# High and low part of the tokens in one matmul: a decoder layer in split precision on one core of Trainium2

## The chip, the core and the metric

The kernel runs on one core of a Trainium2 chip. The core has a matrix engine (TensorE, PE in the profile; its weight loads are shown apart as PEld), three engines for element-wise work (VectorE or DVE, ScalarE or ACT, GpSimd or POOL) and a queue that issues most transfers (SyncE, SP). Matmuls read on-chip memory and write accumulators that lie in eight banks of 512 float32 values in each of 128 partitions. Each engine carries out its own instructions in the order in which the program writes them, and waits for others by semaphores. The metric is device time in microseconds (us), lower is better. Before the change three runs took 393.45 to 395.39, with a median of 394.48.

## What is computed

One decoder layer over 256 tokens of width 1024, float32, with 256 memory tokens: half of the first projection goes through a causal pooling mixer, the other half through self-attention with 8 heads of 64 (256 tokens are one block, so it is plain causal attention); then cross-attention with 4 heads of 256 into the memory, then a gated feed-forward layer of width 2816. Each of the three parts ends in a residual sum and a layer normalisation.

```python
z = h @ w_in[l]
u, q, k, v = ...          # 512 columns each
pool_out = multiscale_pool(u, w_pool[l], pool_scale[l])
attn_out = moba_attention(q, k, v).reshape(B_, S_, ATTN_WIDTH)
mix = jnp.concatenate([pool_out, attn_out], axis=-1) @ w_out[l]
h = layer_norm(DEEPNORM_ALPHA * h + mix, ln1_g[l], ln1_b[l])
h = layer_norm(DEEPNORM_ALPHA * h + memory_cross_attention(h, mem, w_xq[l], w_xkv[l], w_xo[l]), ...)
h = layer_norm(DEEPNORM_ALPHA * h + swiglu(h, w_gate[l], w_up[l], w_down[l]), ...)
```

## The kernel before

**Split precision.** Every large product is made of three matmuls of a faster, rounded float32 type (fp32r). A matrix is split into a high part (a rounded copy, made by ACT) and a low part (what rounding left, made by DVE); the three products are high x high, high x low and low x high, and low x low is left out. They are summed in one accumulator.

**Weights.** `Stream` (L42) brings weights in pieces of 512 KB, numbered w0, w1, ... in the order of their use. `fetch` issues the transfer, and `prepare` makes the high part on ACT (L79) and the low part on DVE (L80). `get` prepares what is asked for and, unless `held` is set, one more piece, up to six ahead (`AHEAD`). There are four raw buffers and eight pairs of prepared ones. Other transfers hang on pieces through `before`: the transposed tokens `xr`, the memory `mr`, the residual `xt`, the norms' parameters. w0 to w8 belong to q and k, w9 to w12 to v, w13 to w16 to u, w17 to w24 to the memory's keys.

**Two kinds of product.** In `proj_rows` and `proj_n` a block of tokens is stationary, and high and low part of the weights stream past it. In `proj_t` and `product_qk` a block of 128 x 128 weights is stationary and the 256 tokens stream, so that the result comes out transposed. For each block of weights these issue three matmuls of 256 columns: high weights with high tokens, high weights with low tokens, low weights with high tokens. High and low tokens lie in two separate tiles (`xT`, `mT`, `cT`, `h1T`, `h2T`, ...), each of 8 blocks of 256 tokens.

**Accumulators.** Two pools share the eight banks: `accbank` gives one of four single banks for long products, `bank` one of four for everything else (scores, transposes, attention). A transposed product of 256 channels fills one bank: two times 256 tokens.

**The order.** It is written out by hand. After q and k (`product_qk`, L315, emptied by `keep_qk`, L303) the generators `do_v`, `do_u` and `do_xk` (L446 to L467) are advanced step by step (`run(v, 2)` makes two steps), and the pieces of self-attention are put in between: `scores` (L373, scores, mask, row maximum on DVE, exponentials on ACT, scaling on DVE), `probs_t` (L395, transposes of the probabilities and their copies, one on DVE, one on ACT), `attend` (L411), then `windows` (L424, on POOL), `pool_diff` and `mix_pool` for pooling. What leaves an accumulator is issued when its generator is advanced past its last step: u's first half, for instance, is copied (L457) after `scores(1, 1)` and `attend(1)`, as its sixteenth step lies behind them. The cross-attention follows the same pattern: `do_xq` (L619) makes the queries of one head, split into high and low by L280 and L281, and `xscores` of that head comes five or six steps into the next head's queries. Gate and up (L730) are ten rounds of two transposed products; `project` (L564) makes the three products that end in a residual sum.

Of the kernel before, what the change touches and what calls it, by code (L numbers as in the profile page):

```python
# [14 lines left out]
P = 128  # L15
# [18 lines left out]
PR_BUFS = 6  # L34
BUSY = 13
# [68 lines left out]
def decoder_layer(  # L104
# [8 lines left out]
    pa = ctx.enter_context(tc.tile_pool(name="pacc", bufs=4, space=bass.MemoryType.PSUM))  # L113
# [5 lines left out]

    def bank(name):  # L120
# [29 lines left out]
    xT = (a8("xTh", F32R), a8("xTl", F32R))  # L150
    mT = (a8("mTh", F32R), a8("mTl", F32R))
# [6 lines left out]
    def load_xt(k, n=2):  # L158
        nc.sync.dma_start(xr[:, k:k + n, :], x_t[:, k:k + n, :])

    def split_xt(k, n=2):
        split(xT[0][:, k:k + n, :], xT[1][:, k:k + n, :], xr[:, k:k + n, :])
# [7 lines left out]
    def split_mem(k):  # L170
        split(mT[0][:, k:k + 4, :], mT[1][:, k:k + 4, :], mr[0][:, k:k + 4, :])
# [56 lines left out]
    def proj_t(pss, numbers, yT, last=True):  # L228

        for f in range(2):  # L230
            for k in range(KD):
                hi, lo = ws.get(numbers, k)
                s = slice(f * P, (f + 1) * P)
                three(pss[f], (hi[:, s], lo[:, s]), pair(yT, ALL, k), k == 0, k == KD - 1)
                if f == 1 and last:
                    ws.done(numbers, k)
                yield

    def proj_n(ps, numbers, yT, t, last=True):

        for k in range(KD):
            three(ps, pair(yT, ALL, k, slice(t * P, (t + 1) * P)), ws.get(numbers, k), k == 0, k == KD - 1)
# [4 lines left out]
    def proj_rows(acc, chunks, get, pieces, first, last, free):  # L247
# [3 lines left out]
        for numbers in chunks:  # L251
            nk = ws.rows(numbers)
            for t in sorted({piece[0] for piece in pieces}):
                for j in range(nk):
                    k = k0 + j
                    y = pair(get(k), ALL, slice(t * P, (t + 1) * P))
# [26 lines left out]
    def transpose_tok(dst, tok, t, k0):  # L283
# [5 lines left out]
        split(dst[0][:, k0:k0 + 4, ts], dst[1][:, k0:k0 + 4, ts], ps.rearrange("p (k t) -> p k t", k=4))  # L289
# [11 lines left out]
    qk = [accbank(f"pqk{i}").rearrange("p (f t) -> p f t", f=2) for i in range(4)]  # L301

    def keep_qk(i):  # L303

        dst = qkT[:, 2 * i:2 * i + 2, :]
        if i == 0:
            nc.scalar.mul(dst, qk[i], HD ** -0.5)
        elif i == 1:
            nc.vector.tensor_scalar(dst, qk[i], HD ** -0.5, None, op0=OP.mult)
        elif i == 2:  # L310
            nc.scalar.copy(dst, qk[i])
        else:
            nc.vector.tensor_copy(dst, qk[i])

    def product_qk(k):  # L315
        for i in range(4):
            j, c0 = divmod(i, 2)
            hi, lo = ws.get(c_qk[k], j)
            for f in range(2):
                s = slice((2 * c0 + f) * P, (2 * c0 + f + 1) * P)  # L320
                (ya, yb), (wa, wb) = pair(xT, ALL, k), (hi[:, s], lo[:, s])
                for n, (w, y) in enumerate(((wa, ya), (wa, yb), (wb, ya))):
                    nc.tensor.matmul(qk[i][:, f, :], w, y, start=k == 0 and f == 0 and n == 0,  # L323
                                     stop=k == KD - 1 and n == 2, skip_group_check=True)
            if k == KD - 1:
                keep_qk(i)
# [33 lines left out]
    def scaled(dst, sm):  # L360
        nc.vector.reciprocal(sm, sm)  # L361
        for j in range(2):
            nc.vector.tensor_scalar(dst[:, j, :], dst[:, j, :], sm[:, j:j + 1], None, op0=OP.mult)  # L363
# [9 lines left out]
    def scores(hq, t):  # L373
# [15 lines left out]
        for pr, sm in todo:  # L389
            scaled(pr, sm)  # L390

    cT = (a8("cTh", F32R), a8("cTl", F32R))
# [18 lines left out]
    def attend(hp):  # L411
# [7 lines left out]
        split(cT[0][:, 4 + hp, :], cT[1][:, 4 + hp, :], po[:, :S])  # L419
# [18 lines left out]
    def mix_pool(g):  # L438
        pm = bank("pm")
        nc.tensor.matmul(pm[:, :S], wpl[:, g, :], upad[:, g, PADW:], start=True, stop=True)  # L440
        nc.scalar.activation(cT[0][:, g, :], pm[:, :S], AF.Copy, bias=0.0, scale=psc[:, g:g + 1])
        nc.vector.scalar_tensor_tensor(cT[1][:, g, :], pm[:, :S], psc[:, g:g + 1],
                                       r32(cT[0][:, g, :]), op0=OP.mult, op1=OP.subtract)
# [358 lines left out]
```

## Time and profile before

| | us |
|---|---|
| median of three runs | 394.48 (393.45 to 395.39) |
| the profiled execution | 393.67 |
| its span, first to last instruction | 391.6 |
| TensorE busy in it | 381.3 (97%) |
| VectorE busy | 244.6 (62%) |
| ScalarE busy | 176.1 (45%) |
| transfers | 72.0 MB, 184 GB/s on average |

The mean clock granted to TensorE is 0.996 of full speed. In the timelines that follow, a row has the start in us, the length in us, the engine, the line of the kernel, the operation, result and operands by the names of the program, shapes, type and count; what stands in brackets is how long the engine was idle before, and what ended that. Recorded lengths of matmuls overlap. Rows of stages begin with the stretch in us, then its length, the busy time of PE, PEld, DVE, ACT and POOL with the number of instructions, the granted clock, the share of the DMA engines and GB/s.

### The profile page before, as it was taken

Reading aid. Unit: us, or ns where it says so; the run is one execution under the profiler, and the core shown is the slowest. Engines: PE = TensorE matmul, PEld = TensorE weight load, DVE = VectorE, ACT = ScalarE, POOL = GpSimd, SP = SyncE. Lnnn points to the kernel's source line nnn. Section 1 sums busy time; section 2 is a strip of 40 time slices with the busy share of each in tenths; the row PEclk is TensorE's granted clock in tenths of the full one; section 3 lists DMA queues with packets and bytes.
Section 4 is the critical chain, followed back from the end, with each engine's and each line's share of the span. In section 5 each row is a group of like instructions: output and inputs, shape, how many; then the busy total and the mean of one; then the engine's idle time right before and its main releaser. Section 6 shows DMA issues by size and latency. Waiting matters only on the chain.

```text
span 391.6 us, 6504 instructions
## 1 busy us (share of the span) xinstructions
PE 381.3 (97%) x2651; PEld 353.6 (90%) x2651; DVE 244.6 (62%) x327; ACT 176.1 (45%) x253; POOL 31.0 (8%) x37
## 2 busy tenths in 40 slices
PE   8999999999999999999999999999999999999991
PEld 7997889898888899988899999999999998888881
DVE  2749998776388766656887744556644457543276
ACT  3745848455233645455245633355543335343000
POOL 1000006500420000001400000000000000000022
PEclk9999999999999999999999999999999999999998
DMA  7998544756606862234408756654445875753002
GB/s 239 336 329 273 200 166 148 273 174 228 236 9 220 281 251 109 110 107 161 162 3 279 241 177 216 216 179 173 144 170 197 277 258 163 256 175 108 1 27 82
DMA packets 21886, 71.99 MB, mean 184 GB/s; under 512 B 2784, under 2 KB 3552, under 8 KB 21728
## 3 DMA queue, kind: packets, MB, share of 16 engines
q1 hardware_dynamic: 21568, 71.05, 52.7%
q10 hardware_dynamic: 288, 0.52, 0.7%
q8 instruction: 21, 0.34, 0.3%
q14 instruction: 9, 0.07, 0.1%
HBM read 70.52 MB, written 1.05 MB: 183 GB/s over the span
## 4 chain that ended last, share of the span: by engine, by line
PE 95%; DMA 2%; DVE 1%; SPq 0%; ACT 0%; issue 0%; DVEq 0%
PE acc L220 9%; PE acc L219 9%; PE acc L221 9%; PE pu L219 6%; PE pu L220 6%; PE pu L221 6%; PE pqk L323 5%; PE pg L220 5%; PE pg L219 5%; PE pg L221 5%; PE pxk L219 2%; PE pxq L219 2%; PE pxq L221 2%; PE pxq L220 2%; PE pxk L220 2%; PE pxk L221 2%
## 5 line engine op out<-in xcount | busy, mean ns | idle before, releaser
L739 DVE TENSOR_TENSOR sgt<-sgt,pu 128x512 f32<-128x512 f32 x10 | 6.9, 688 | 42.4 <-PE pu L221 42.4
L276 ACT CAST gTh<-sgt 128x512 fp32r<-128x512 f32 x10 | 6.2, 620 | 56.5 <-DVE sgt L739 56.5
L537 POOL TENSOR_TENSOR rs<-rs,mhalf 128x1 f32<-128x1 f32 x6 | 5.5, 912 | 199.0 <-DVE rs L536 199.0
L526 DVE SCALAR_TENSOR_TENSOR r<-h,acc 128x256 f32<-128x256 f32 (+1 forms) x12 | 6.0, 502 | 11.5 <-PE acc L221 11.5
L356 ACT ACTIVATE pr<-pr,mx 128x128 f32<-128x128 f32 (+1 forms) x16 | 7.2, 449 | 11.0 <-DVE mx L367 10.7
L547 ACT ACTIVATE r<-r,rs 128x384 f32<-128x384 f32 x2 | 1.2, 616 | 22.8 <-POOL rs L537 22.8
L277 DVE TENSOR_TENSOR gTl<-sgt,gTh 128x512 fp32r<-128x512 f32 x10 | 6.9, 693 | 6.9 <-ACT gTh L276 6.9
L541 DVE SCALAR_TENSOR_TENSOR r<-r,mv,g 128x512 f32<-128x512 f32 (+2 forms) x14 | 10.7, 776 | 0.0
L356 ACT ACTIVATE xpr<-xs,mx 128x256 f32<-128x256 f32 x8 | 3.7, 469 | 12.4 <-DVE mx L367 12.4
L529 DVE BATCH_NORM_STATS2 st<-r 128x6 f32<-128x512 f32 (+1 forms) x16 | 9.0, 561 | 0.5
L429 POOL TENSOR_TENSOR win<-upad 128x271 f32<-128x271 f32 x4 | 3.6, 888 | 59.9 <-DVE pr L363 59.9
L80 POOL TENSOR_TENSOR w59l<-w59r,w59h 128x1024 fp32r<-128x1024 f32 x1 | 2.4, 2442 | 69.9 <-ACT w59h L79 69.9
L276 ACT CAST h2Th<-tp 128x512 fp32r<-128x512 f32 x4 | 2.3, 587 | 12.3 <-PE tp L287 12.3
L738 ACT ACTIVATE sgt<-pg 128x512 f32<-128x512 f32 x10 | 6.0, 596 | 3.6 <-PE pg L221 3.6
L552 DVE SCALAR_TENSOR_TENSOR h<-r,rs,b 128x512 f32<-128x512 f32 x8 | 6.0, 752 | 1.9 <-POOL rs L537 1.8
L277 DVE TENSOR_TENSOR xTl<-xr,xTh 128x512 fp32r<-128x512 f32 (+1 forms) x5 | 2.9, 580 | 6.2 <-ACT xTh L276 6.2
L429 POOL TENSOR_TENSOR win<-win 128x269 f32<-128x269 f32 (+2 forms) x6 | 6.7, 1118 | 0.5
L526 DVE SCALAR_TENSOR_TENSOR r<-xt,acc 128x512 f32<-128x512 f32 x4 | 2.7, 682 | 6.2 <-PE acc L221 6.2
L361 DVE RECIPROCAL sm<-sm 128x2 f32<-128x2 f32 x12 | 2.0, 165 | 5.9 <-ACT xpr L356 4.5
L367 DVE TENSOR_REDUCE mx<-xs 128x2 f32<-128x512 f32 x4 | 2.8, 691 | 4.4 <-PE xs L221 4.4
L79 ACT CAST w41h<-w41r 128x1024 fp32r<-128x1024 f32 x1 | 1.1, 1051 | 9.5 <-PE tp L287 9.5
L287 PE MATMUL tp<-ident,h 128*128 128x128 f32 x32 | 4.8, 274 | 0.1
(1075 smaller groups left out, 1661.8 us busy)
## 6 DMA issues: line engine op xcount, KB each, us to landing
g<-in_ln_g SPq DMA_DIRECT2D x3, 512.0 KB, 6.3
b<-in_ln_b SPq DMA_DIRECT2D x3, 512.0 KB, 6.9
mr<-in_mem_t SPq DMA_DIRECT2D x1, 1024.0 KB, 7.9
xt<-in_x SPq DMA_DIRECT2D x1, 1024.0 KB, 9.0
out<-r SPq DMA_DIRECT2D x4, 256.0 KB, 2.0
xr<-in_x_t SPq DMA_DIRECT2D x3, 256.0 KB, 6.3
w2r<-in_w_in SPq DMA_DIRECT2D x1, 512.0 KB, 7.0
w3r<-in_w_in SPq DMA_DIRECT2D x1, 512.0 KB, 7.8
```

What stands on the lines that cost most here:

```text
L219: nc.tensor.matmul(ps, wa, ya, start=start, stop=False)
L220: nc.tensor.matmul(ps, wa, yb, start=False, stop=False)
L221: nc.tensor.matmul(ps, wb, ya, start=False, stop=stop)
L276: nc.scalar.copy(h, ps)
L277: nc.vector.tensor_sub(l, ps, r32(h))
L323: nc.tensor.matmul(qk[i][:, f, :], w, y, start=k == 0 and f == 0 and n == 0, stop=k == KD - 1 and n == 2, skip_group_check=True)
L356: nc.scalar.activation(dst[:, j, :], src[:, j, :], AF.Exp, bias=mx[:, j:j + 1], scale=1.0, accum_out=sm[:, j:j + 1])
L429: nc.gpsimd.tensor_add(nxt[:, 2 * n - 1:], cur[:, 2 * n - 1:], cur[:, n - 1:PADW + S - n])
L526: nc.vector.scalar_tensor_tensor(self.r[:, s], self.tok[:, s], ALPHA, acc, op0=OP.mult, op1=OP.add)
L529: nc.vector.bn_stats(self.st[:, self.n, :], self.r[:, c0:c1])
L541: nc.vector.scalar_tensor_tensor(self.r[:, s], self.r[:, s], self.mv[:, 0:1], gb[self.i][0][:, s], op0=OP.subtract, op1=OP.mult)
L739: nc.vector.tensor_mul(sg, sg, pu)
```

## The change

- **One matmul for high and low tokens.** High and low tokens of one block now lie side by side (`HighLow`), so that high weights meet all 512 columns in one matmul (`apart`). Its result fills one bank: high x high in the first half, high x low in the second. Low weights then meet the high tokens, 256 columns, added into the second half. So there are two matmuls for three, wherever weights are stationary (q and k, u, the memory's keys, the queries of cross-attention, gate and up without their first 256 columns). Products with stationary tokens keep their three.
- **Accumulators.** A transposed product of 256 channels now fills two banks. `accbanks` gives one of two pairs of banks; `bank` stays as it was. q's products use both pairs, k's the four single banks.
- **Leaving an accumulator** (`total`): ACT copies the second half to an on-chip tile (`co`, two of them), and DVE adds the first half to it. What came before (copy, scaling, split, activation) works on the sum. The q and k products lose `keep_qk`; u, the memory's keys, the queries of cross-attention, gate and up each get `total`.
- **Self-attention.** The scaling of the probabilities in `scores` moves from DVE to ACT (`scaled(pr, sm, True)`); v makes four steps ahead of the first scores, not two.
- **First loads.** On the SyncE queue: first token block, second token block, w2; the third and fourth block are issued by ACT, behind the preparation of w0. w1 is prepared ahead of the second token block. 16 transposes keep TensorE busy at the start, not 13.
- **Buffers.** Five tiles for probabilities and the like, not six; the first gate and up products use `bank`.

```diff
-PR_BUFS = 6
-BUSY = 13
+PR_BUFS = 5
+BUSY = 16
+CO_BUFS = 2
...
-    pa = ctx.enter_context(tc.tile_pool(name="pacc", bufs=4, space=bass.MemoryType.PSUM))
+    pa = ctx.enter_context(tc.tile_pool(name="pacc", bufs=2, space=bass.MemoryType.PSUM))
...
+    class HighLow:
+        def __init__(self, name):
+            self.tiles = [ap.tile([P, KD // 2, 2, S], F32R, tag="a8", name=f"{name}{i}") for i in range(2)]
...
+        def __call__(self, k, ts=slice(None)):
+            t, j = self.tiles[k // 4], k % 4
+            return t[:, j, 0, ts], t[:, j, 1, ts]
+        def both(self, k):
+            return self.tiles[k // 4][:, k % 4].rearrange("p a s -> p (a s)")
...
-    def accbank(name):
-        return pa.tile([P, 512], F32, tag="acc", name=name)
+    def accbanks(name):
+        return pa.tile([P, 2, 512], F32, tag="acc", name=name)
...
+    def apart(ps, w, y, k, first, last):
+        nc.tensor.matmul(ps, w[0], y.both(k), start=first, stop=False, skip_group_check=True)
+        nc.tensor.matmul(ps[:, S:], w[1], y(k)[0], start=False, stop=last, skip_group_check=True)
...
-                three(pss[f], (hi[:, s], lo[:, s]), pair(yT, ALL, k), k == 0, k == KD - 1)
+                apart(ps[f], (hi[:, s], lo[:, s]), yT, k, k == 0, k == KD - 1)
...
+    def total(dst, ps, scale=None):
+        co = small("co")
+        whole = not isinstance(ps, list)
+        for f in (slice(0, 2),) if whole else (0, 1):
+            p = ps[:, f] if whole else ps[f]
+            main, rest = p[..., :S], p[..., S:]
+            if scale is None:
+                nc.scalar.copy(co[:, f], rest)
+                nc.vector.tensor_add(dst[:, f], main, co[:, f])
+            else:
+                nc.scalar.mul(co[:, f], rest, scale)
+                nc.vector.scalar_tensor_tensor(dst[:, f], main, scale, co[:, f], op0=OP.mult, op1=OP.add)
+        return dst
...
-                keep_qk(i)
+                total(qkT[:, 2 * i:2 * i + 2, :], qk[i], HD ** -0.5 if i < 2 else None)
...
     load_xt(0, 1)
+    ws.fetch(2, nc.scalar)
     load_xt(1, 1)
-    ws.fetch(2, nc.scalar)
-    load_xt(2)
+    ws.fetch(3, nc.sync)
     split_xt(0, 1)
     ws.prepare(1)
+    load_xt(2, 2, nc.scalar)
+    ws.prepare(2)
     split_xt(1, 1)
-    ws.prepare(2)
...
         for pr, sm in todo:
-            scaled(pr, sm)
+            scaled(pr, sm, True)
...
-        acc = {piece: accbank("pv") for piece in pieces}
+        pv = accbanks("pv")
+        acc = {piece: pv[:, piece[0]] for piece in pieces}
...
-            ps = accbank("pu").rearrange("p (f t) -> p f t", f=2)
-            yield from proj_t([ps[:, f, :] for f in range(2)], c_u[c], xT)
-            nc.scalar.copy(upad[:, 2 * c:2 * c + 2, PADW:], ps)
+            ps = accbanks("pu")
+            yield from proj_t(banks(ps), c_u[c], xT)
+            total(upad[:, 2 * c:2 * c + 2, PADW:], ps)
...
-            split(xkT[0][:, 2 * c:2 * c + 2, :], xkT[1][:, 2 * c:2 * c + 2, :], ps)
+            split(*xkT.blocks(2 * c, 2), total(small("xk"), ps))
...
-    run(v, 2)
+    run(v, 4)
     scores(0, 0)
...
-        ps = (bank if h == 0 else accbank)("pxq").rearrange("p (f t) -> p f t", f=2)
-        yield from proj_t([ps[:, f, :] for f in range(2)], c_xq[h], h1T)
+        ps = [bank("pxq") for f in range(2)] if h == 0 else accbanks("pxq")
+        yield from proj_t(banks(ps), c_xq[h], h1T)
         xqT[h] = [sp.tile([P, 2, S], F32R, name=f"xq{i}", tag="pr", bufs=PR_BUFS) for i in range(2)]
-        split_scaled(*xqT[h], ps, 256 ** -0.5)
+        split(*xqT[h], total(small("xq"), ps, 256 ** -0.5))
...
-        pg = accbank("pg").rearrange("p (f t) -> p f t", f=2)
-        pu = bank("pu").rearrange("p (f t) -> p f t", f=2)
-        run(proj_t([pg[:, f, :] for f in range(2)], c_gu[c][0], h2T))
+        pg = accbanks("pg")
+        run(proj_t(banks(pg), c_gu[c][0], h2T))
...
-        run(proj_t([pu[:, f, :] for f in range(2)], c_gu[c][1], h2T))
         sg = sp.tile([P, 2, S], F32, name="sgt", tag="pr", bufs=PR_BUFS)
-        nc.scalar.activation(sg, pg, AF.Silu, bias=0.0, scale=1.0)
-        nc.vector.tensor_mul(sg, sg, pu)
+        total(sg, pg)
+        nc.scalar.activation(sg, sg, AF.Silu, bias=0.0, scale=1.0)
+        pu = accbanks("pu")
+        run(proj_t(banks(pu), c_gu[c][1], h2T))
+        su = sp.tile([P, 2, S], F32, name="sut", tag="pr", bufs=PR_BUFS)
+        nc.vector.tensor_mul(sg, sg, total(su, pu))
```

More of the change, by code (lines that the diff above doesn't have):

```diff
@@ L149, in decoder_layer @@
     xt = ap.tile([P, T, D], F32, tag="a8", name="xt")
[L150 to L151 removed]
+    xT, mT = HighLow("xT"), HighLow("mT")
     def load_x():
@@ L299, in keep_busy @@
             nc.tensor.transpose(ps[:, :P], ident, ident)
[L301 to L313, printed above, removed]
+    qk = [accbanks(f"pqk{i}") for i in range(2)] + [[bank(f"pqk{i}{f}") for f in range(2)] for i in (2, 3)]
     def product_qk(k):
@@ L320, in product_qk @@
                 s = slice((2 * c0 + f) * P, (2 * c0 + f + 1) * P)
[L321 to L324, printed above, removed]
+                apart(banks(qk[i])[f], (hi[:, s], lo[:, s]), xT, k, k == 0, k == KD - 1)
             if k == KD - 1:
-                keep_qk(i)
+                total(qkT[:, 2 * i:2 * i + 2, :], qk[i], HD ** -0.5 if i < 2 else None)
         for j in range(2):
@@ L576, in project @@
         for piece in pieces:
-            yield from proj_rows(acc, rest, lambda k: get(done + k), [piece], not head, True, piece == pieces[-1])
+            yield from proj_rows(acc, rest, lambda k, ts: get(done + k, ts), [piece], not head, True, piece == pieces[-1])
             yield piece, acc[piece]
@@ L679, in decoder_layer @@
     xattend(3)
-    h2T = (a8("h2Th", F32R), a8("h2Tl", F32R))
-    gT = [(a8(f"gTh{i}", F32R), a8(f"gTl{i}", F32R)) for i in range(3)]
+    h2T = HighLow("h2T")
+    gT = [HighLow(f"gT{i}") for i in range(3)]
     norm = Norm(2, h1[:, 0, :], h2[:, 0, :])
```

81 lines of the change are left out of this document (46 added, 35 removed).

## The prediction

> **What bounds the kernel now.** The page was read first (busy shares, chain that ended last), then the timeline of TensorE (PE), then the timelines of VectorE (DVE) and ScalarE (ACT) from 28 to 62 us and around 148 us, then TensorE's clock at the end of the span.
>
> ```profile
> PE 381.3 (97%) x2651; PEld 353.6 (90%) x2651; DVE 244.6 (62%) x327; ACT 176.1 (45%) x253; POOL 31.0 (8%) x37
> ...
> PE 95%; DMA 2%; DVE 1%; SPq 0%; ACT 0%; issue 0%; DVEq 0%
> ```
>
> TensorE is busy nearly all the time and the chain lies on it for 95%. So a matmul made cheaper is worth its full saving, and a wait put in front of one costs its full length. What matmuls cost is the distance between starts, as their recorded lengths overlap:
>
> ```profile
> 239.80 0.28 PE L219 MATMUL pu<-h2Th,w71h 128*128 128x256 f32 x1
> 241.84 0.28 PE L221 MATMUL pu<-h2Th,w72l 128*128 128x256 f32 x1
> ...
> 326.74 0.40 PE L219 MATMUL acc<-w102h,gTh 128*128 128x512 f32 x1
> 327.44 0.28 PE L219 MATMUL acc<-w102h,gTh 128*128 128x256 f32 x1
> 328.15 0.40 PE L219 MATMUL acc<-w103h,gTh 128*128 128x512 f32 x1
> ```
>
> From 239.80 to 241.84 lie 17 distances: 0.120 us for one of 256 columns. From 326.74 three of 512 columns take 0.70, 0.233 each, and then six of 256 take 0.71, 0.118 each: widths can alternate without a loss.
>
> **Term 1, fewer and wider matmuls.** Three matmuls of 256 columns become one of 512 and one of 256. A triple took 3 x 0.120 = 0.360 and will take 0.233 + 0.118 = 0.351: it saves 9 ns. There are 544 triples: 64 for q and k, 32 for u, 64 for the memory's keys (pxk), 64 for the cross-attention's queries (pxq), 320 for gate and up. Those of q, k and u end in waits that something else sets (Term 2), so 448 count: 448 x 0.009 = 4.0 us off. The trace has no 512-column matmul whose result is two halves of a bank, the second half then added to. At worst it costs what the two it replaces cost (no saving); at best 0.229, the lower end of what rounding leaves of 0.70 / 3, and the triple saves 13 ns, 5.8 us. I take 9 ns, as the row of mixed widths is nearest.
>
> [...]
>
> **Term 2, from the first loads to the memory's keys.** The result now lies in two halves; to leave the bank, ACT copies one half and DVE adds the other to it. And the accumulators are two pairs of banks where there were four single ones: a new product must wait until the pair used two products earlier has passed through ACT and DVE. Both engines work strictly in the order written, behind weight preparation and softmax. The rows below are picked from the timelines in order of time.
>
> ```profile
> 11.53 0.39 PE L323 MATMUL pqk<-xTh,w2l 128*128 128x256 f32 x1 [0.57 <-DVE w2l L80]
> 28.38 1.05 ACT L79 CAST w11h<-w11r 128x1024 fp32r<-128x1024 f32 x1 [2.73 <-DMA w11r<-in_w_in]
> 29.67 1.05 ACT L79 CAST w12h<-w12r 128x1024 fp32r<-128x1024 f32 x1 [0.24 <-DMA w12r<-in_w_in]
> 30.75 1.23 DVE L80 TENSOR_TENSOR w12l<-w12r,w12h 128x1024 fp32r<-128x1024 f32 x1
> 31.54 0.40 PE L219 MATMUL pv<-w9h,xTh 128*128 128x512 f32 x1
> 31.89 0.68 DVE L309 TENSOR_SCALAR qkT<-pqk 128x512 f32<-128x512 f32 x1
> 33.09 0.39 DVE L349 TENSOR_SCALAR fac<-cnt 128x16 f32<-128x16 f32 x4
> 36.19 0.42 DVE L385 TENSOR_TENSOR pr<-ps,tri 128x256 f32<-128x256 f32 x1
> ```
>
> The reordered loads bring w2 forward, for whose low part TensorE waits 0.57 us at 11.53; with the half-speed time before it I put that at 1 us. But q's accumulators leave behind w12's preparation, and w12 waits for its load at 29.67: the start's gain ends in this queue. Loads are late there whatever the start does, so I take w12 0.5 us earlier (0 to 1). Then w12l ends at 31.5, the first addition (0.68) at 32.2, and only then may v's product start: 32.2, against 31.54. Before, ACT alone emptied that bank, and DVE gave two operations (L309, L313) in 1.2 us, 31.89 to 33.09. Now DVE gives two of 512 columns (0.60 apart) and four of 256 (0.35 apart), 2.6. So the softmax's first addition moves from 36.19 by -0.5 + 1.5 to 37.2.
>
> ```profile
> 38.29 0.39 ACT L356 ACTIVATE pr<-pr,mx 128x128 f32<-128x128 f32 x1
> 39.40 0.68 DVE L385 TENSOR_TENSOR pr<-ps,tri 128x512 f32<-128x512 f32 x1
> 42.67 0.49 ACT L356 ACTIVATE pr<-pr,mx 128x256 f32<-128x256 f32 x1
> 43.16 1.04 ACT L79 CAST w15h<-w15r 128x1024 fp32r<-128x1024 f32 x1
> 47.65 0.68 DVE L405 COPY sb<-pt 128x512 f32<-128x512 f32 x1
> 49.11 0.38 ACT L406 COPY sb<-pt 128x256 f32<-128x256 f32 x1
> 49.54 0.66 PE L417 MATMUL po<-sb,vt 128*64 128x256 f32 x4
> ```
>
> The scaling of the probabilities moves from DVE to ACT. Without it DVE comes to the second softmax 2.75 instead of 3.2 us after the first: 39.95. Its exponentials end 3.8 later (39.40 to 43.16), 43.75. Then ACT has four scalings of 256 columns; no row shows one, the exponential of that size (0.49) is nearest, 0.41 apart as issued to 0.50 one after the other; four are 1.75: 45.5. Only then w15h, at 43.16 before: +2.35. From w15h to the copy that ends at 49.49 nothing changes in ACT's queue, so both copies of the transposed probabilities (47.65 on DVE, 49.11 on ACT) move by 2.35 too, and the product that reads the second (49.54) starts at 51.9.
>
> ```profile
> 51.18 0.41 DVE L385 TENSOR_TENSOR pr<-ps,tri 128x256 f32<-128x256 f32 x1
> 53.66 0.35 ACT L276 CAST cTh<-po 128x256 fp32r<-128x256 f32 x1
> 57.26 0.68 DVE L385 TENSOR_TENSOR pr<-ps,tri 128x512 f32<-128x512 f32 x1
> 60.99 0.19 ACT L356 ACTIVATION_READ_ACCUMULATOR pr<-pr,mx 128x1 f32 x1
> 61.13 0.28 PE L219 MATMUL pxk<-mTh,w17h 128*128 128x256 f32 x1
> 61.34 0.58 ACT L457 COPY upad<-pu 128x512 f32<-128x512 f32 x1
> ```
>
> The third softmax starts 2.35 later, at 53.5, and its exponentials end 2.5 after (51.18 to 53.66), 56.05. Four scalings of 128 columns (0.31 to 0.40 each, 1.35) put cTh at 57.4, 3.75 later than 53.66. Everything up to the fourth softmax hangs on it: 57.26 becomes 61.0. Exponentials end 3.92 after (57.26 to 61.18), 64.9; four scalings, 66.65; cTh, 66.9; u's first half copied by ACT (0.58), 67.45; added by DVE (0.68), 68.15. Now pxk's first product, at 61.13 before, needs the pair of banks that u's first half held. Before, u's copy at 61.34 came as late, but pxk had a bank of its own. So pxk starts at 68.2: +7.1. TensorE would be there at 63.1 (61.13 + 2.35 - 32 x 0.009) and stands for 5 us. The bounds are +6.2 (loads 1 us earlier, short scalings) and +8.1 (no earlier, 0.50 for each). What follows, pooling included, moves along; the weights have been ready for long.
>
> **Term 3, the cross-attention's queries.**
>
> ```profile
> 147.80 0.28 PE L219 MATMUL pxq<-h1Th,w45h 128*128 128x256 f32 x1
> 148.00 0.60 ACT L280 ACTIVATE xq<-pxq 128x512 fp32r<-128x512 f32 x1 [1.27 <-PE pxq L221]
> 148.62 0.69 DVE L281 SCALAR_TENSOR_TENSOR xq<-pxq,xq 128x512 fp32r<-128x512 f32 x1 [0.64 <-ACT xq L280]
> 149.60 0.28 PE L219 MATMUL xs<-xkTh,xq 128*128 128x256 f32 x1
> ```
>
> Head 1's product ends as 147.80 starts; ACT and DVE then take until 149.31, covered by five steps of the next head (1.8 us). Two operations became four: ACT, DVE, ACT, DVE, to about 150.7. With five steps at 0.351 the scores come at 149.56, and their third matmul, the first that needs the low part, at 149.8: 0.9 lost. Head 0 leaves bank by bank, the first early, and loses 0.4. Head 2 has six steps and loses 0.55, or 0.85 if weight preparation is ahead of it. Head 3 is covered by two other stages. I take 2.1 (1.3 to 2.8).
>
> At no cost: gate and up (10 x 2 more operations on ACT and on DVE, each 0.6 to 0.7 us; the pair is needed again only after another product's 5.6 us, without which each would cost 1.4); w_down's accumulators for the second 128 tokens (2.8 us of matmuls for the first ahead of them, without which 1.5); 3 more warming transposes (before the first load lands; 0.6 otherwise); five tiles of probabilities for six, and high and low parts side by side (the sixth waits for transposes that are written ahead of it anyway, and the same elements are written).
>
> **Sum.** -4.0 + 7.1 + 2.1 = +5.2. The profiled execution took 393.67, of which 391.6 are its span; that becomes 398.9. The median of the runs shown, 394.48, lies 0.81 above it, so 399.7 is forecast.
>
> **Rivals.** (a) *The clock falls during the 5 us.*
>
> ```profile
> 6.47 0.41 PE L323 MATMUL pqk<-xTh,w0h 128*128 128x256 f32 x1
> 7.54 0.41 PE L323 MATMUL pqk<-xTh,w0l 128*128 128x256 f32 x1
> ...
> 383.00:384.00 1.00, 0.71 (x6) 0.51 (x5) 0.58 (x2) 0.00 (x0) 0.00 (x0) 1.00 0.00 0
> 388.00:389.00 1.00, 0.00 (x0) 0.00 (x0) 0.52 (x2) 0.00 (x0) 0.02 (x1) 0.89 0.69 262
> 389.00:390.00 1.00, 0.00 (x0) 0.00 (x0) 0.00 (x0) 0.00 (x0) 0.00 (x0) 0.50 0.54 207
> ```
>
> At the start a 256-column matmul takes 0.214 (6.47 to 7.54, five distances), 56% of the later speed. The last matmul ends near 383.7, and the granted clock is 0.50 from about 388.8: 5.1 us of idling halve it. The 5 us of Term 2 lie on that edge, and an earlier fall costs what the start paid, some 5 us of matmuls at 56%, 2.2 us: 401.9. For it: two shorter waits of about 1 to 2.5 us (before v and before the scores at 49) come ahead of it. Against: everything between is dense. [...]
>
> (b) *The queues catch up: faster.* ACT and DVE reach u's addition by 61, so that pxk never waits. It decides if the chain of Term 2 gains the 7 us back between 37 and 61. For it: DVE gives 16 scalings away, and TensorE has fewer matmuls. Against: the chain is one of hand-overs, in which DVE waits for ACT's scalings instead. Then 544 - 64 cold or covered triples save 4.3, the start 1.0; with Term 3 the time is 394.48 - 5.3 + 2.1 = 391.3, and 389.2 if the queries' copies are hidden too.
>
> (c) *Half of the wait.* ACT's scalings overlap better, or loads come earlier, and pxk waits 2 us and not 5: the chain moves by 3.5, and 394.48 - 4.0 + 3.5 + 2.1 = 396.1.
>
> (d) *The change doesn't give what it says:* a 512-column matmul into two halves takes what two did. No term 1: 403.7. Against it stand the 0.233 rows.
>
> **How the numbers follow.** The forecast, 399.7, has 0.43; its own range from its bounds is 394.48 - 5.8 + 6.2 + 1.3 = 396.2 to 394.48 + 8.1 + 2.8 = 405.4. (a) has 0.18, (b) 0.20 (two fifths of it below 390), (c) 0.12, (d) 0.07. From 390 to 404 leaves out that part of (b), 0.08, and of (d) and the forecast's upper end about 0.07. About 0.5%, 2 us, is what a measurement of this kernel can tell from no change: faster (below 392.5) is (b), 0.20; the same (392.5 to 396.5) most of (c), 0.10; slower the rest, 0.70.
>
> **What would show it.** Term 1: distances of 0.231 to 0.235 and 0.118 to 0.120 in gate and up, ten rounds of 11.2 us where there were 11.5. Term 2: v's first product at about 32 behind the first qkT addition; scaling groups of 0.3 to 0.5 us on ACT; a gap of some 5 us ahead of the first pxk, ended by DVE's addition into upad, pxk at 67 to 69. Term 3: gaps of 0.4 to 0.9 before the score matmuls of heads 0 to 2. Rival (a): distances of 0.2 just behind the gap. If pxk starts before 63, or those gaps are absent, the step that failed is the order of ACT's and DVE's queues as summed in Term 2; if the distances do not change, Term 1.

## The result, and the profile after

| | before | after |
|---|---|---|
| median of the runs | 394.50 us (393.45 to 395.39) | 418.81 us (416.55 to 420.25) |
| profiled execution, its span | 393.67, 391.6 us | 416.55, 414.5 us |
| mean granted clock in it | 0.996 | 0.984 |

The changed kernel is slower by 6.1%: the ratio is 1.0612, with a 95% interval from 1.0548 to 1.0676. The forecast had the sign and not the size: +5.2 us were forecast, the profiled execution shows +22.9. The page of the changed kernel, its busy times and its chain of waits:

```profile
PE 384.0 (93%) x2110; PEld 326.0 (79%) x2110; DVE 263.0 (63%) x346; ACT 198.6 (48%) x302; POOL 30.0 (7%) x37
...
PEclk9999997999989999999999999999999999999998
...
PE 71%; DVE 14%; ACT 6%; DMA 5%; issue 2%; POOL 0%; ACTq 0%; DVEq 0%
```

TensorE has 541 instructions fewer, yet the chain lies on it for 71% and no longer for 95%: VectorE and ScalarE now decide in between. In the clock's row two slices fell to 7 and 8 tenths (the 8 of the last slice, where TensorE has nothing left to do, stands before the change too). To see where the time went, the span is cut at the first matmul of each stage, read from TensorE's timeline of both kernels:

| from the first matmul of ... | before, us | after, us | difference | forecast |
|---|---|---|---|---|
| q and k to v's | 26.82 | 28.39 | +1.57 | |
| v to the memory's keys (pxk) | 29.59 | 35.14 | +5.55 | +7.1 with the row above |
| the keys to the product with w_out | 28.22 | 30.08 | +1.86 | -0.6 |
| w_out to the memory's values (xv) | 21.79 | 27.63 | **+5.84** | 0 |
| the values to the queries (pxq) | 23.70 | 23.71 | 0.01 | 0 |
| the queries to the product with w_xo | 31.56 | 34.54 | +2.98 | +1.5 |
| w_xo to the first gate and up | 27.57 | 30.23 | **+2.66** | 0 |
| first gate and up | 13.22 | 13.21 | -0.01 | 0 |
| ten rounds of gate and up | 115.41 | 113.28 | -2.13 | -2.9 |
| w_down to its last matmul | 60.84 | 65.40 | **+4.56** | 0 |
| the rest | 8.16 | 8.21 | +0.05 | 0 |

The three bold rows, 13.06 us together, are in no term of the forecast. They are the three products that go through `project`. The list of waits, each with its total, its count and its longest:

```profile
PE acc L238 <- DVE r L561: 10.0, 6, 3.1
...
PE pxk L249 <- DVE upad L275: 4.3, 1, 4.3
```

Six times TensorE stood for VectorE's L561, the sum of a norm (residual plus accumulator). The timelines of TensorE and of VectorE at w_out show how:

```profile
111.69 0.39 PE L240 MATMUL acc<-w32h,cT 128*128 128x512 f32 x1
112.85 0.50 PE L238 MATMUL acc<-w29h,cT 128*128 128x512 f32 x1 [0.78 <-DVE r L561]
...
115.71 0.39 PE L238 MATMUL acc<-w29h,cT 128*128 128x512 f32 x1
...
118.21 0.39 PE L240 MATMUL acc<-w32h,cT 128*128 128x512 f32 x1
121.72 0.80 PE L238 MATMUL acc<-w29h,cT 128*128 128x512 f32 x1 [3.12 <-DVE r L561]
122.31 0.63 PE L239 MATMUL acc<-w29l,cT 128*128 128x512 f32 x1
122.74 0.63 PE L240 MATMUL acc<-w29h,cT 128*128 128x512 f32 x1
```

```profile
112.11 0.69 DVE L561 SCALAR_TENSOR_TENSOR r<-xt,acc 128x512 f32<-128x512 f32 x1 [3.17 <-PE acc L240]
...
115.91 0.69 DVE L561 SCALAR_TENSOR_TENSOR r<-xt,acc 128x512 f32<-128x512 f32 x1 [2.38 <-PE acc L240]
116.64 0.69 DVE L564 BATCH_NORM_STATS2 st<-r 128x6 f32<-128x512 f32 x1
...
117.68 0.74 DVE L576 SCALAR_TENSOR_TENSOR r<-r,mv,g 128x512 f32<-128x512 f32 x1
...
120.32 0.75 DVE L587 SCALAR_TENSOR_TENSOR h<-r,rs,b 128x512 f32<-128x512 f32 x1
120.98 0.68 DVE L561 SCALAR_TENSOR_TENSOR r<-xt,acc 128x512 f32<-128x512 f32 x1
```

The last two weight chunks are run piece by piece: (first tokens, left half), (first, right), (second, left), (second, right). The first piece ends behind 111.69. The second lies in the other half of the same pair of banks, and starts only when the sum at 112.11 has read the first. The third, at 115.71, lies in the other pair and starts at once. The fourth again shares a pair, and the third's sum is queued on VectorE behind the whole first norm (statistics, two centrings, two scalings, from 116.64 on): it comes at 120.98, and TensorE stands for 3.12 us by its bracket, 3.3 if counted from start to start less the usual distance. (Stops told without a bracket are counted from start to start in what follows, and come out some 0.15 us longer.) Behind it matmuls lie 0.43 us apart where 0.227 is usual: the granted clock is 0.50 from 121.2 to 124.6. The same two stops come at w_xo (behind 202.52 and 210.63) and at w_down (behind 389.15 and 398.89). In the kernel before each piece had a bank of its own, and the sums there read one bank while TensorE wrote the next without a stop. The first piece's last matmul and the second's first two, and the sum of the first:

```profile
102.75 0.39 PE L221 MATMUL acc<-w32h,cTl 128*128 128x512 f32 x1
102.98 0.39 PE L219 MATMUL acc<-w29h,cTh 128*128 128x512 f32 x1
103.20 0.39 PE L220 MATMUL acc<-w29l,cTh 128*128 128x512 f32 x1
```

```profile
103.18 0.69 DVE L526 SCALAR_TENSOR_TENSOR r<-xt,acc 128x512 f32<-128x512 f32 x1 [4.87 <-PE acc L221]
```

The third piece's sum was as late there (110.97, behind the same norm), and nothing waited for it. So the unit of these waits (0.78 and 3.12 us) is the tile of two banks that the program declares, not the bank.

The stop that the forecast did see, in TensorE's timeline, and the clock around it in a view by windows (busy time and count of PE, PEld, DVE, ACT and POOL, then the granted clock):

```profile
63.65 0.28 PE L250 MATMUL pu<-xT,w16l 128*128 128x256 f32 x1
68.21 0.79 PE L249 MATMUL pxk<-mT,w17h 128*128 128x512 f32 x1 [4.28 <-DVE upad L275]
68.80 0.41 PE L250 MATMUL pxk<-mT,w17l 128*128 128x256 f32 x1
69.02 0.63 PE L249 MATMUL pxk<-mT,w17h 128*128 128x512 f32 x1
```

```profile
64.00:66.00 2.00, 0.00 (x0) 0.00 (x0) 0.22 (x2) 1.99 (x7) 0.00 (x0) 1.00 0.19 78
66.00:68.00 2.00, 0.00 (x0) 0.00 (x0) 0.96 (x2) 2.00 (x5) 0.00 (x0) 0.65 0.00 0
68.00:70.00 2.00, 1.79 (x5) 1.59 (x6) 1.75 (x3) 2.00 (x4) 1.61 (x2) 0.50 0.00 0
```

pxk starts at 68.21, as forecast, and at half clock: rival (a) came true as well.

### The profile page after: what moved, and what is told of

It reads as the page before. It is cut to its first block, busy times and chain, and to the rows that moved or that the text cites. A ratio compares the mean times of both kernels' runs of the same rounds, so it can differ in the third digit from the quotient of the medians.

```text
span 414.5 us, 5454 instructions
## 1 busy us (share of the span) xinstructions
PE 384.0 (93%) x2110; PEld 326.0 (79%) x2110; DVE 263.0 (63%) x346; ACT 198.6 (48%) x302; POOL 30.0 (7%) x37
## 4 chain that ended last, share of the span: by engine, by line
PE 71%; DVE 14%; ACT 6%; DMA 5%; issue 2%; POOL 0%; ACTq 0%; DVEq 0%
PE pu L249 9%; PE pg L249 9%; PE acc L238 8%; PE acc L239 7%; PE acc L240 7%; PE pu L250 5%; PE pg L250 5%; PE pxk L249 4%; DMA xr<-in_x_t 2%; PE pxk L250 2%; DMA w12r<-in_w_in 2%; DVE r L561 2%; PE xv L240 2%; PE xv L239 2%; PE xv L238 2%
## 5 line engine op out<-in xcount | busy, mean ns | idle before, releaser
L561 DVE SCALAR_TENSOR_TENSOR r<-h,acc 128x256 f32<-128x256 f32 (+1 forms) x12 | 6.0, 504 | 17.1 <-PE acc L240 17.1
L274 ACT COPY co<-pu 128x512 f32<-128x512 f32 x12 | 7.0, 585 | 16.6 <-PE pu L250 16.6
L321 ACT CAST gT<-sgt 128x512 fp32r<-128x512 f32 x10 | 6.2, 621 | 15.1 <-DVE sgt L777 15.1
L275 DVE TENSOR_TENSOR sut<-pu,co 128x512 f32<-128x512 f32 x10 | 6.9, 691 | 8.7 <-ACT co L274 8.7
L322 DVE TENSOR_TENSOR gT<-sgt,gT 128x512 fp32r<-128x512 f32 x10 | 6.9, 693 | 6.9 <-ACT gT L321 6.9
L274 ACT COPY co<-pg 128x512 f32<-128x512 f32 x10 | 5.9, 586 | 9.3 <-PE pg L250 9.3
L773 ACT ACTIVATE sgt<-sgt 128x512 f32<-128x512 f32 x10 | 6.3, 632 | 8.3 <-DVE sgt L275 8.3
L321 ACT CAST h2T<-tp 128x512 fp32r<-128x512 f32 x4 | 2.3, 586 | 15.0 <-PE tp L332 15.0
L561 DVE SCALAR_TENSOR_TENSOR r<-xt,acc 128x512 f32<-128x512 f32 x4 | 2.7, 686 | 9.3 <-PE acc L240 9.3
L275 DVE TENSOR_TENSOR sgt<-pg,co 128x512 f32<-128x512 f32 x10 | 6.9, 691 | 1.9 <-ACT co L274 1.9
L249 PE MATMUL pxk<-mT,w17h 128*128 128x512 f32 x8 | 4.1, 534 | 4.3 <-DVE upad L275 4.3
L777 DVE TENSOR_TENSOR sgt<-sgt,sut 128x512 f32<-128x512 f32 x10 | 6.9, 692 | 0.3
```

Source lines behind the costliest of these rows:

```text
L249: nc.tensor.matmul(ps, w[0], y.both(k), start=first, stop=False, skip_group_check=True)
L274: nc.scalar.copy(co[:, f], rest)
L275: nc.vector.tensor_add(dst[:, f], main, co[:, f])
L321: nc.scalar.copy(h, ps)
L561: nc.vector.scalar_tensor_tensor(self.r[:, s], self.tok[:, s], ALPHA, acc, op0=OP.mult, op1=OP.add)
```

## The experiments

All run times of this section stand against 418.81 us after and 393.98 to 394.39 us before (the kernel before was run again each time); stages are named as in the table.

### 1. Neighbouring pieces in different pairs

```diff
-            acc[piece] = (two[piece[0]][:, n % 2] if n < 4 else bank("acc"))[:, :piece[2] - piece[1]]
+            acc[piece] = (two[n % 2][:, n // 2] if n < 4 else bank("acc"))[:, :piece[2] - piece[1]]
```

> Only the pairing of accumulators in the row-major projections changes: neighbouring pieces lie in different pairs, so that a piece's sum is read while the other pair is written. Theory (a wait on the whole pair): the six stops of TensorE for a norm's sum (behind 111.69, 118.21, 202.52, 210.63, 389.15 and 398.89 us) go, and with them the half clock behind the second; the three stages that lost 5.8, 2.7 and 4.6 us come back to their lengths of before (21.8, 27.6, 60.8 us), less up to 0.6 us where the memory's values now wait for the third piece's sum: 12.5 us off, 404.0 us in the profiled run. Rival (the norm's chain on VectorE is what is late, and the pair only shows it): the stop moves to the fourth piece and under 4 us come off: 412 to 415.

Measured: 406.85 us (405.30 to 407.29), ratio to before 1.0313 (1.0285 to 1.0341): 12.0 us off the median, where 12.5 was expected of the profiled run. The six stops are gone. The stages took 23.47, 27.57 and 61.89 us: w_xo is back at its old length, the others keep 1.7 and 1.0. What stays are three new stops. Since the second pair is now written from the first step on, and no longer 2.7 us later, it is waited for at w_out (0.92 us, for the addition of the last keys) and at w_down (0.92, for the addition of the last up product); and the values wait for the third piece's sum:

```profile
122.67 0.47 PE L238 MATMUL xv<-w33h,mT 128*128 128x512 f32 x1 [0.50 <-DVE r L561]
```

The instructions are the same and in the same order; only which two pieces share a tile differs. So the wait on the whole pair is the cause: of the 13.06 us the three stages give back 10.3 here, and what is left are the new stops, waits for a pair again. They go as well where pieces 1 and 3 have single banks (experiment 8, with other edits beside it: 21.79, 27.53 and 60.83 us). The norm's chain costs TensorE nothing by itself.

### 2. The addition of u ahead of the last softmax

```diff
     split_mem(4)
-    run(u, 3)
+    run(u, 6)
     scores(1, 1)
```

> Three more steps of u go ahead of the last scores, so that u's first half is added before the last softmax is queued on ScalarE and VectorE. Theory (pxk waits for the pair only because the addition stands behind that softmax): pxk starts near 64 us and not at 68.2, its matmuls are at full speed from the first; 4.4 us of wait and 1.9 of half clock go, and 1 to 2 come back as a wait of the transposes of the last probabilities, which are as late as before: 3.5 to 6 us off, 410.5 to 413 in the profiled run. Rival (softmax and scaling are the bound, the pair only the first to show it): the wait moves whole to the transposes and to pxk's second product, under 2 us off.

Measured: 415.54 us (414.57 to 416.56), 3.3 off the median, a little under the lowest expected (the profiled execution, 416.56, gained nothing, since w_down ran longer in it, see the last section). pxk starts 31.01 us behind v's product and not 35.14, without a stop and at full clock. But the next stage takes 30.60 us, where it takes 27.64 without a stop or a fall of the clock (experiment 3), by stops that had been hidden behind the first:

```profile
67.02 0.27 PE L434 MATMUL pt<-ident,pr 128*128 128x128 f32 x1
68.38 0.33 PE L435 MATMUL pt<-ident,pr 128*128 128x128 f32 x1 [1.08 <-ACT pr L395]
```

ScalarE's scalings (L395) are late for the transposes, and the pooling's product is late by another 0.99 us. Theory and rival each hold in part: the pair was the first to show a chain that is late as a whole.

### 3. TensorE kept busy in the stop

```diff
     run(u)
+    keep_busy(36)
     run(xk, 6)
```

> 36 transposes of the identity into a spare bank stand between u and the memory's keys; nothing else changes and the wait for the pair stays. Theory (the clock halves because TensorE idles there): pxk still starts at 68.2 us, but its matmuls are 0.235 and 0.118 us apart from the first, and 1.9 us come off: 414.6 in the profiled run. Rival (the matmuls behind the stop are slow for want of weights or of the memory's tokens): spacing of 0.42 and 0.22 us stays, no change.

Measured: 416.52 us (415.68 to 418.30), 2.3 off the median. TensorE's timeline:

```profile
65.15 4.09 PE L344 MATMUL busy<-ident 128*128 128x128 f32 x36
69.66 0.50 PE L249 MATMUL pxk<-mT,w17h 128*128 128x512 f32 x1 [0.42 <-DVE upad L275]
70.00 0.28 PE L250 MATMUL pxk<-mT,w17l 128*128 128x256 f32 x1
70.11 0.40 PE L249 MATMUL pxk<-mT,w17h 128*128 128x512 f32 x1
70.35 0.28 PE L250 MATMUL pxk<-mT,w17l 128*128 128x256 f32 x1
```

pxk waits for the same addition (the whole start lies 1.0 us later here), but its matmuls are 0.235 and 0.117 us apart from the second on, and its stage takes 27.64 us instead of 30.08. So half the clock behind the stop cost 2.4 us; 2.2 was the price in rival (a).

### 4. The wide matmul taken apart

```diff
-        nc.tensor.matmul(ps, w[0], y.both(k), start=first, stop=False, skip_group_check=True)
+        nc.tensor.matmul(ps[:, :S], w[0], y(k)[0], start=first, stop=False, skip_group_check=True)
+        nc.tensor.matmul(ps[:, S:], w[0], y(k)[1], start=False, stop=False, skip_group_check=True)
```

> The wide matmul is taken apart again: three matmuls of 256 columns, into the same two halves of a bank, all else as in the changed kernel. Theory (the traces' rows: a triple of 0.354 us against 0.361): gate and up take 115.4 us for ten rounds and not 113.3, the cross-attention's queries and the memory's keys 0.4 us more each: 2.5 to 3 us longer than the changed kernel. Rival (the forecast's 9 ns): 4 us longer. Rival (the wide matmul gives nothing, gate and up gained by the additions moved off the path): no change.

Measured: 419.95 us (418.64 to 420.27), 1.1 above the median after, with ranges that overlap. Gate and up take 115.41 us, to the last digit what they took before the change, so a triple costs 0.3607 us as three and 0.354 as two: 6.7 ns. The queries' stage grew by only 0.14, since stops there take the rest up.

### 5. Wide matmuls alone

```diff
-        run(proj_t(banks(pg), c_gu[c][0], h2T))
+        run(proj_t(banks(pg), c_gu[c][0], h2T, low=c % 2 == 0))
```

The same for up; with `low` false the second matmul of `apart` isn't issued.

> In every second round of gate and up the product of the weights' low part is left out, so that only wide matmuls remain there. Theory (changing between 512 and 256 columns costs): wide matmuls 0.227 us apart, as in the projections that have only those, a round of 32 of them 7.26 us. Rival (a wide matmul of this kind costs 0.235 by itself): 7.5 us.

One run, 404.42 us. The wide matmuls of one such round, and for comparison the changed kernel's pairs of wide and narrow:

```profile
229.94 1.07 PE L249 MATMUL pg<-h2T,w62h 128*128 128x512 f32 x4
230.85 1.07 PE L249 MATMUL pg<-h2T,w61h 128*128 128x512 f32 x4
231.76 1.07 PE L249 MATMUL pg<-h2T,w62h 128*128 128x512 f32 x4
```

```profile
249.73 0.40 PE L249 MATMUL pu<-h2T,w68h 128*128 128x512 f32 x1
249.97 0.28 PE L250 MATMUL pu<-h2T,w68l 128*128 128x256 f32 x1
...
251.85 0.40 PE L249 MATMUL pg<-h2T,w70h 128*128 128x512 f32 x1
```

Alone, eight wide matmuls take 1.82 us, 0.228 each. In pairs, six wide and six narrow take 2.12, 0.353 a pair, and a wide one is 0.235 to 0.24. So a pair costs 5 to 7 ns more than a wide and a narrow one in stretches of their own (0.228, and 0.118 to 0.120). A change of width by itself isn't shown to be the reason: in w_down, where three wide and six narrow ones follow each other, the prediction's rows have 1.41 us for nine, 0.01 more than 3 x 0.228 + 6 x 0.12. The loss shows where every matmul changes width, and its cause stays open. A whole round as expected (7.26 us) can't be read, since such short rounds wait for ScalarE and VectorE.

### 6. The scaling back on VectorE

```diff
-            scaled(pr, sm, True)
+            scaled(pr, sm)
```

> Only the scaling of the self-attention's probabilities goes back from ScalarE to VectorE. Theory (the scalings on ScalarE put 2.35, 1.35 and 1.75 us into the chain to u's addition, and VectorE does them beside the exponentials): pxk starts 3 us earlier against the first product of v, 32.1 us behind it and not 35.1. Rival (VectorE is as late itself): 34.6 or more.

One run, 412.58 us. pxk starts 32.10 us behind v's product, 3.0 earlier, the number expected, and its stop is short:

```profile
65.57 0.28 PE L250 MATMUL pu<-xT,w16l 128*128 128x256 f32 x1
66.72 0.51 PE L249 MATMUL pxk<-mT,w17h 128*128 128x512 f32 x1 [0.87 <-DVE upad L275]
```

The clock doesn't fall there, and the keys' stage takes 27.65 us. So the scaling on ScalarE was 3.0 of the 5.55 us that the stage from v to the keys lost, and of the 7.1 of Term 2.

### 7. More cover for the queries

```diff
-    run(xq[1], 5)
+    run(xq[1], 9)
     xscores(0)
     run(xq[1])
-    run(xq[2], 5)
+    run(xq[2], 9)
     xscores(1)
-    run(xq[2], 6)
+    run(xq[2], 3)
     xprobs_t(0)
     run(xq[2])
-    run(xq[3], 6)
+    run(xq[3], 9)
     xscores(2)
     xattend(0)
-    run(xq[3], 6)
+    run(xq[3], 4)
```

> Only more steps of the next head's queries ahead of the scores: 9, 9 and 9 where there were 5, 5 and 6. Theory (the stops of 0.91 + 0.39, 0.75 + 0.39 and 0.69 + 0.39 us are the four hand-overs of a head's queries, and 1.4 us more of matmuls covers them): the stage from the queries to the second projection takes 31.0 to 31.4 us and not 34.5. Rival (weight preparation gets in between and eats the cover): 32.5 or more.

One run, 416.33 us. The stage takes 32.82 us, 1.7 less: the rival's 32.5 or more, and for the rival's reason. VectorE prepares weights between ScalarE's copy for head 1, at 164.22, and its own addition to it:

```profile
164.35 1.23 DVE L81 TENSOR_TENSOR w49l<-w49r,w49h 128x1024 fp32r<-128x1024 f32 x1
165.50 0.69 DVE L278 SCALAR_TENSOR_TENSOR xq<-pxq,co 128x512 f32<-128x512 f32 x1
```

At head 2 it is w51l, at 172.37. Stops of 0.28 and 0.39 stay at heads 1 and 2, for the low parts (head 0 has none), and a new one of 0.83 us comes at the second attention product, for the low part of its probabilities.

### 8. Versions without the waits

Five edits together: pieces 1 and 3 of w_out and w_down in single banks (w_xo as in experiment 1), the edits of 2, 6 and 7, and two weight chunks prepared behind q and k:

```diff
-    two = [accbanks("acc") for t in range(T)]
+    two = [accbanks("acc") for t in range(1 if single else T)]
...
+        own = n > 3 or single and n % 2
+        acc[piece] = (bank("acc") if own else two[n % 2][:, n // 2])[:, :piece[2] - piece[1]]
...
-        ws.held = k == KD - 1
+        ws.held = k >= KD - 2
```

> Five edits together: the odd pieces of the first and last row-major projections in single banks and the middle one's pairs crossed; u's first half added before the last softmax; probabilities scaled on VectorE again; four, four and three more steps of cover for the cross-attention's queries; the preparation of two weight chunks held back until q and k have left their banks. Theory (all that was lost is waits for a pair of banks, and waits of one order): stages in order 27.3, 29.5, 28.2, 21.8, 23.7, 31.3, 27.6, 13.2, 113.3, 60.9 and 8.2 us behind 4.7: a span of 389.7, a profiled run of 391.8, below the kernel before by 0.5%. Rival (the added copies and additions load ScalarE and VectorE so that some wait always remains): 395 us or more.

Measured: 394.23 us (393.49 to 395.09), ratio 1.0005 (0.9990 to 1.0020): no difference from the kernel before, and between what the theory and the rival gave. w_out, w_xo and w_down take 21.79, 27.53 and 60.83 us, as before or less, gate and up 113.28. Two stages missed: v to the keys 30.81 (29.5 expected) and the queries 32.81 (31.3). What gate and up gain, 2.1 us against the kernel before, is given back there. A second order of the same edits (three chunks held back, the pooling factors behind the second scores, the first scores one step earlier, cover of 10, 10 and 9, the second head's transposes earlier):

> The five edits, the order shifted further where stops were left: three weight chunks held back behind q and k, the pooling factors computed behind the second scores, scores of the first block one step of v earlier and of the second in the same place, cover of 10, 10 and 9 steps for the queries, the second head's transposes right behind the first attention product. Theory (what is left is order alone): v's product starts 0.6 us earlier than with the five edits, the stage from v to the memory's keys takes 29.6 and not 30.8 us, the queries' 31.4 and not 32.8: 3 us below them, 391.2 us, 0.7% below the kernel before. Rival (VectorE and ScalarE are too full around 30 to 60 us, stops move on): 393 to 394.5.

Measured: 394.49 us (393.64 to 396.38), ratio 1.0005 (0.9989 to 1.0021). The rival: the queries' stage took 32.20 us, but v to the keys 31.54, longer than in the first order. The stops moved on. The same kernel with the wide matmul taken apart as in experiment 4:

> The same with the wide matmul taken apart into two of 256 columns. Theory (where TensorE is the bound everywhere, the 6.7 ns for a triple that gate and up showed hold for all 544): 3.6 us longer, 2.1 of it in gate and up. Rival (only gate and up gain, elsewhere stops take it up): 2.1 to 2.5 us longer.

Measured: 397.75 us (396.92 to 398.38), ratio 1.0086 (1.0064 to 1.0109). Where TensorE is the bound almost everywhere, the wide matmul is worth 3.3 us by the medians, between the theory's 3.6 and the rival's 2.1 to 2.5; in the two profiled executions, whose starts differ, it is 2.2, and 2.13 of that lies in gate and up.

Last, q and k go back to three matmuls into single banks (as the kernel before had them), so that only one engine empties each. Loads look like what bounds them (in the prediction's rows ScalarE waits for w11 and w12). Other edits as in the second order, without its changes to chunks, factors and first scores; the warming transposes write a pair of accumulators, as q and k fill the single banks:

```diff
-    qk = [accbanks(f"pqk{i}") for i in range(2)] + [[bank(f"pqk{i}{f}") for f in range(2)] for i in (2, 3)]
+    qk = [bank(f"pqk{i}").rearrange("p (f t) -> p f t", f=2) for i in range(4)]
...
-            total(qkT[:, 2 * i:2 * i + 2, :], qk[i], HD ** -0.5 if i < 2 else None)
+            keep_qk(i)
```

with the first loads in the old order, and in the new:

> q and k go back to three matmuls of 256 columns in single banks that ScalarE and VectorE empty alone, and the first loads to their old order; behind them stand the edits on the projections, u, the scaling and the queries (cover 10, 10, 9). Theory (the wide matmul pays only where TensorE is the bound; at the start loads are, and there its copies and additions only cost): the start takes 26.8 us, v to the memory's keys 29.5, the keys 27.8, the queries 32.2, gate and up 113.3: span 389.2, 391.3 us, 0.7% below the kernel before. Rival (the start's lateness has another cause): 393.5 or more.

> The same with the first loads in the new order. Theory of the forecast (the new order brings w2 forward and gains 1 us until q and k are done): 25.8 us from the first matmul to v's product. Rival (the new order only puts the wait from w2 to w3, as the start's stops of 0.71, 0.63 and 0.76 us at w2 and w3 show): 26.8 to 27.5 us.

Measured: 392.41 us (391.38 to 393.74), ratio 0.9955 (0.9938 to 0.9971), with the old order, and 392.18 (391.38 to 394.92), ratio 0.9958 (0.9939 to 0.9978), with the new. Both beat the kernel before, by 0.4%, and the changed one by 26 us. The profiled execution of the first took 391.38 us, where the theory gave 391.3; its median lies 1.1 above that. Busy times and chain of the first of them:

```profile
PE 377.4 (97%) x2174; PEld 326.6 (84%) x2174; DVE 264.5 (68%) x358; ACT 192.2 (49%) x282; POOL 30.8 (8%) x37
...
PE 92%; DVE 3%; DMA 2%; ACT 1%; issue 0%; SPq 0%; DVEq 0%; ACTq 0%
```

Its stages are 26.68, 29.39, 27.72, 21.79, 23.70, 32.22, 27.53, 13.21, 113.28, 60.83 and 8.16 us: VectorE is as busy as in the changed kernel, but TensorE hardly waits for it. What q and k alone gave isn't shown, as the second order's changes to chunks, factors and first scores went with them. The order of the loads makes no difference that these runs can tell; in the one profile of each, q and k took 26.68 us in the old and 27.66 in the new, where stops at w3 (0.74 and 0.76 us) join that at w2 (0.76 in both). The 1 us that the forecast gave the new order doesn't show.

## Why the prediction was right or wrong

**Term 2 held, nearly point by point.** The first softmax was forecast at 37.2 and came at 37.96, the third at 53.5 (54.00), the fourth at 61.0 (61.25), u's addition ended at 68.15 (68.15), pxk started at 68.2 (68.21). Only the beginning was off: v's product started at 33.07 and not at 32.2, as the start gained nothing. Shorter scalings (1.16 us for four of 128 columns and 1.60 for four of 256 until ScalarE's next operation starts, where 1.35 and 1.75 were taken) gave back 0.5 of the 0.76 us by which the first softmax was late. That the errors cancel to a hundredth at pxk is luck; the path is not. Experiment 6 shows the part of it that is scaling, 3.0 us. One slip in the working changed nothing: by its own terms rival (c) moves the chain by 4.1 us and not 3.5 (396.7).

**Term 1 had its mechanism and the wrong size.** A triple saves 6.7 ns and not 9: over the 448 counted, 3.0 us and not 4.0. The 0.233 us came from a row in which one wide matmul in three is followed by a narrow one; in the change each one is, and experiment 5 shows what such pairs cost. "Widths can alternate without a loss" held for such rows only.

**Term 3 was too small.** With its 64 triples' 0.4 us taken out, the queries' stage lost 3.4 us where 2.1 was the term. Head 0 was put at 0.4, as it leaves bank by bank; it lost 1.3, the most, because its rounding to the high part and the subtraction after it wait for both banks. In each head the third score matmul waited another 0.39 us for the low part:

```profile
164.52 0.69 DVE L278 SCALAR_TENSOR_TENSOR xq<-pxq,co 128x512 f32<-128x512 f32 x1 [0.64 <-ACT co L277]
...
165.25 0.62 ACT L321 CAST xq<-xq 128x512 fp32r<-128x512 f32 x1 [0.76 <-DVE xq L278]
...
165.90 0.69 DVE L322 TENSOR_TENSOR xq<-xq,xq 128x512 fp32r<-128x512 f32 x1 [0.68 <-ACT xq L321]
```

With ScalarE's copy ahead of them these are four operations, each starting some 0.7 us behind the last; they make 2.8 us from the product's end to 166.6.

**Rival (a) came true, beside the forecast and not instead of it.** It was priced well (2.2 us; 2.4 by experiment 3) and given 0.18, because the one idle stretch that was read, at the end of the span, kept its clock for 5.1 us. Here the clock fell 2.6 us into the stop. How it fell in the other stops stands in the last section.

**The step that failed is in the list "at no cost".** It let the paired accumulators pass with "w_down's accumulators for the second 128 tokens (2.8 us of matmuls for the first ahead of them, without which 1.5)". That is right in kind for the moment at which a pair is taken over (experiment 1, which removes this cover, pays 0.92 us for it), and it was the only moment considered. The end of the same products, where pieces are finished one after another and each is read by a norm's sum while the next is to be written, was not looked at, though two of the four pieces share a tile there, in three products. That is 13.06 us of the 22.9, of which some 1.5 are matmuls at half clock behind 121.72. With it, the clock's 2.4, and Terms 1 and 3 as measured, the sum is -3.0 + 7.1 + 3.4 + 2.4 + 13.1 = 23.0, against 22.9 in the profiled execution.

## What to carry to other kernels

When accumulators are joined into one tile of several banks, list for each of them both the writer that comes next and the reader that is still due, for every product that uses the pool, and not only those the change is about: whatever shared a tile here waited as one (0.78 and 3.12 us at w_out). Pieces that are finished one after another belong in different tiles. A saving of some nanoseconds for a matmul paid where TensorE was the bound (gate and up, 2.1 us); where loads or other engines are, its extra copies are what is left, and the version that left q and k alone was the fastest.

## What the runs showed of the hardware

In these runs the granted clock didn't halve after a fixed idle time. Read from the granted clock by windows, or from the distances of the matmuls behind the stop, in the changed kernel and experiments 2, 3, 4, 6 and 7: of 17 stops of TensorE of 2.1 to 4.3 us, eight saw the clock fall within the stop or with its end, 2.1 to 2.8 us after the last matmul where windows show the moment (2.6 at pxk in the changed kernel, 2.3 at w_out in experiment 7); three just behind it, 3.7 to 4.9 us after that matmul; and six, one of them 3.1 us long (w_out in experiment 4), not at all. At the ends of the spans of the kernel before, the changed one, experiments 6 and 7 and the first version of experiment 8 it fell after 4.7 to 5.1 us. The same stop in w_down, 2.7 us long, halved it in experiment 2 (first view by windows) and not in the changed kernel (second view); the granted clock stands behind POOL's count:

```profile
397.60:398.60 1.00, 0.00 (x0) 0.00 (x0) 0.96 (x3) 0.00 (x0) 0.15 (x1) 1.00 0.70 262
398.60:399.60 1.00, 0.15 (x1) 0.15 (x1) 0.93 (x4) 0.00 (x0) 0.00 (x0) 0.62 0.39 147
399.60:400.60 1.00, 1.00 (x5) 1.00 (x6) 0.26 (x1) 0.00 (x0) 0.00 (x0) 0.50 0.31 115
```

```profile
400.20:401.20 1.00, 0.00 (x0) 0.00 (x0) 0.93 (x4) 0.00 (x0) 0.08 (x1) 1.00 0.69 262
401.20:402.20 1.00, 0.21 (x1) 0.22 (x2) 0.96 (x3) 0.00 (x0) 0.00 (x0) 1.00 0.46 174
402.20:403.20 1.00, 1.00 (x10) 1.00 (x10) 0.19 (x1) 0.00 (x0) 0.00 (x0) 1.00 0.24 88
```

Ten matmuls and not five in the last of these microseconds: w_down took 68.11 us with the fall and 65.40 without. That would fit the changed kernel's four runs (416.55 and 417.45 us at a mean clock of 0.984, 420.18 and 420.25 at 0.976), but no run separates that cause: the last version of experiment 8, which has no such stop, spreads as widely (391.38 to 394.92). In these runs stops of 2.5 us were not safe: one of that length, ahead of v's product in experiment 2, halved the clock.
